# Residual rows loaded ahead of a quarter's last products, and wide weights issued by GpSimd, both in written order

## The chip, the cores and the metric

One core of a Trainium2 chip runs the whole kernel. The metric is the device time of one execution in microseconds (us), as the median of several runs; 1192.09 us for the kernel before, from three runs. A profiled execution gives one more time, its own, and a trace of every instruction. PE is TensorE, DVE VectorE, ACT ScalarE, POOL GpSimd, and SP is SyncE, which here does nothing but issue DMA transfers. POOL can issue transfers too; it then does so between its own computations.

## The reference

Two decoder layers over 1024 tokens of 1024 channels, with 256 memory tokens. Each layer projects its input, forms a main branch and a branch that attends into the memory, gates both, projects them back and normalizes the sum with the scaled input, the residual:

```python
def mixer_sublayer(x, mem, w_in, w_mem_kv, w_out, main_fn):
    h = x @ w_in
    u_main = h[..., :D_MAIN]
    q_mem = h[..., D_MAIN:D_MIX]
    g_main = h[..., D_MIX:D_MIX + D_MAIN]
    g_mem = h[..., D_MIX + D_MAIN:]
    y_main = main_fn(u_main)
    y_mem = memory_attention(q_mem, mem, w_mem_kv)
    y = jnp.concatenate([y_main * jax.nn.silu(g_main), y_mem * jax.nn.silu(g_mem)], axis=-1)
    return y @ w_out
...
    y = mixer_sublayer(x, mem, w_in[layer], w_mem_kv[layer], w_out[layer], main_fn)
    x = layer_norm(ALPHA * x + y, ln_g[layer], ln_b[layer])
```

In layer 0 `main_fn` is a causal pooling over windows of 2, 4, 8 and 16 tokens. In layer 1 it is attention with 16 heads of 64 channels, in which a cumulated forget gate is added to the logits; keys, values and gates come from one projection of layer 1's input.

## The kernel before

**Products.** Every f32 operand is split into two parts of lower precision (three with a second copy), and a product is three matmuls. Splitting a weight is work of ACT and DVE, or, while `low[0]` is set (L230, L330), of POOL alone.

**The order of the work.** The program is written for a framework that orders each engine's instructions by a priority of its own, from the order in which they are written and from when it takes their inputs to be ready. An instruction that is ready early, such as a load of weights, can be put far ahead of its place. Two things restrain it: PE's order is the written one in the attention stages (L523, L1229), and an instruction handed to `tc.keep_in_program_order` is put behind the instruction of its engine that was written last. Buffers come from pools: a tag names a shape and the number of buffers, and a load waits until a buffer of its tag is free.

**Heads of layer 1 (`fox`, L1133).** 16 heads run one after the other in eight steps each, one step for every block of 128 queries, from the last block to the first. In a step PE makes the logits (L1026, matmuls in L323), DVE adds the rows of the forget gate and takes the extremum (L1028), ACT exponentiates (L1036), ACT and DVE make two halves (L1064, L1065), and SP turns them by a DMA transpose (L1081, T<-P). Six steps later PE multiplies them with the values (L1090). POOL makes the masked diagonal three steps ahead (L1002).

**The fill.** Between these parts, PE works through projections that later heads need: keys, queries, values and gates of the next pairs. `Fill.pump` (L53) doles them out by columns. Each projection is a `slab` (L325) of 48 matmuls of 512 columns. In the fill, where `low[0]` is set, a slab first asks for its weights as one wide tile of 512 KB (L331, L332, tag B of ten buffers), then splits its first half (L335; on POOL L176, L193, L178, named B<-B, w<-B and w<-B,w), then its second (L338). The three `yield 0` let the fill start these ahead of the slab's own matmuls: the first as soon as the slab is second in line, the others when the slab in front has at most 30 and 16 matmuls left (L59). The keys' slab of each pair and a gate are started by hand in steps 2, 5 and 6 of a pair's second head (L1179 to L1182). There are 27 wide loads, all on SP. In the last pair three late gates (`late_gate`, L1121) are among the fill, and the output weights are fetched and split beside them (L1187 to L1209).

**Weights seen ahead in layer 0.** `look_ahead` (L242) loads weights of layer 1 only to take the largest magnitude. These loads are issued by POOL, in written order (L258, W<-in_win_dram and others).

**Output products and norm (`OutProj.rest`, L615).** The 1024 tokens are four quarters `sp` of 256. For each quarter three groups `c` of four weight tiles follow one another: 2, 0, 1. Each group loads its part of y (L634, T<-y0d or T<-y1d), splits it and runs 48 matmuls (L599). In layer 1 the first two quarters are interleaved. After group 1 `norm` (L650) takes the quarter's two blocks of 128 rows: it gets a G buffer, loads the residual rows (L655: x in layer 0, x1 in layer 1), adds the products to them (L659), takes mean and variance (L660, L662), scales (L670, L672) and stores (L673). In layer 0 it also splits the result into halves and turns them into X (L678). G has four buffers, one of which a piece of the output weights holds during this stage (`PG`, L138).

Of the kernel before, what the change touches and what calls it, by code (L numbers as in the profile page):

```python
# [18 lines left out]
P = 128  # L19
# [53 lines left out]
def run(units):  # L73
    for _ in units:
        pass
# [3 lines left out]
def trunk_kernel(ctx, tc, x, xT, memT, win, wk, wv0, wv, wmk, wmv, wout, poolw, pscale, lng, lnb, bforget, out):  # L79
# [5 lines left out]
    nc = tc.nc  # L85
# [18 lines left out]
    def sb(shape, tag, bufs, dt=F32, where=None):  # L104
        return (where or pool).tile(shape, dt, tag=tag, name=nm(tag), bufs=bufs)

    def ps(shape, tag, bufs):
        return psum.tile(shape, F32, tag=tag, name=nm(tag), bufs=bufs)

    def G(shape=(P, S), dt=F32):  # L110
        return sb(list(shape), "G", 4, dt)

    def T(shape=(P, S), dt=F32R):
        return sb(list(shape), "T", 6, dt)
# [10 lines left out]
    def tiny(n, dt=F32):  # L125
        return small.tile([P, n], dt, tag=f"s{n}{dt}", name=nm("s"), bufs=4 if n < 12 else 2)
# [53 lines left out]
    def parts_of(make, shape):  # L180
        return Split(make(shape), make([shape[0], 2] + list(shape[1:]), BF16))
# [7 lines left out]
    def three(a, b):  # L189
        return (a.hi, b.hi), (a.top, b.lo), (a.lo, b.hi if isinstance(a, Wide) else b.top)  # L190
# [4 lines left out]
    def hi_lo(to, src, pinned=False, top=None):  # L195

        pin = tc.keep_in_program_order if pinned else lambda ins: ins
        pin(nc.scalar.copy(to.hi, src))  # L198
        pin(nc.vector.tensor_tensor(to.lo, src, to.hi.bitcast(F32), ALU.subtract))  # L199
        pin((top or nc.scalar.copy)(to.top, src))  # L200
# [8 lines left out]
    def split_w(src_dram, shape, sc=None, r=None, pin=lambda ins: ins):  # L209
        if r is None:  # L210
            r = raw(shape)
            nc.sync.dma_start(r, src_dram)
        if sc is not None:
            to = half_of(wt, shape)
            if low[0]:
                gp_scaled_hi_lo(to, r, sc)
            else:
                scaled_hi_lo(to, r, sc, pin)
            return to
        to = parts_of(wt, shape)  # L220
        (gp_hi_lo if low[0] else hi_lo)(to, r)
        return to
# [102 lines left out]
    def slab(pieces_dram, X, evac, banks=("pj", 2), g=0):  # L325

        arrived = isinstance(pieces_dram, list)
        sc = sws[g] if isinstance(X, Half) else None
        both = (None, None)
        if low[0]:  # L330
            wide = roomy[0]([P, 2, 4, P])  # L331
            nc.sync.dma_start(wide, pieces_dram.rearrange("c p k m -> p c k m"))  # L332
            both = wide[:, 0], wide[:, 1]
            yield 0
        ws = list(pieces_dram) if arrived else [split_w(pieces_dram[0], [P, 4, P], sc, both[0])]  # L335
        if low[0]:
            yield 0
            ws.append(split_w(pieces_dram[1], [P, 4, P], sc, both[1]))  # L338
            yield 0
        accs = {}  # L340
        high, low_top = (0,), (1, 2)
        if sc is not None:
            order = [(n, pc, (0, 1, 2)) for n in range(2) for pc in range(2)]
        elif arrived:
            order = [(n, pc, part) for pc in range(2) for n, part in ((0, high), (1, high), (1, low_top), (0, low_top))]
        else:
            order = [(0, pc, part) for part in (high, low_top) for pc in range(2)]
            order += [(1, pc, part) for part in (low_top, high) for pc in range(2)]
        seen = {0: 0, 1: 0}
        for n, pc, part in order:  # L350
            if len(ws) <= pc:
                ws.append(split_w(pieces_dram[pc], [P, 4, P], sc, both[pc]))
            if n not in accs:
                accs[n] = ps([P, NH], *banks)
            for i in part:
                a, b = three(ws[pc], X)[i]
                for k in range(4):
                    seen[n] += 1
                    nc.tensor.matmul(  # L359
                        accs[n], a[:, k, :], b[:, pc * 4 + k, n * NH : (n + 1) * NH],  # L360
                        start=seen[n] == 1, stop=seen[n] == 3 * KT,
                    )
                    if seeing[0]:
                        seeing[1] += 1
                        if seeing[1] % 8 == 0:
                            look_ahead()
                    if seen[n] == 3 * KT:
                        evac(slice(n * NH, (n + 1) * NH), accs[n])
                    yield NH
# [174 lines left out]
    class OutProj:  # L544
# [70 lines left out]
        def rest(self, resid, X, dst):  # L615
            order = [(sp, c) for sp in range(ST // 2) for c in (2, 0, 1)]
            accs, splits, gb = {}, [24], []
            if self.accs:
                accs[0], order[:6], splits = self.accs, [(0, 0), (1, 2), (0, 1), (1, 0), (1, 1)], [16, 24]
            if X is not None:  # L620
                self.split(splits.pop())

            def loads():

                for v in (lng, lnb):
                    t = sb([P, D], "P", 4)
                    nc.sync.dma_start(t, v[self.l].partition_broadcast(P))
                    gb.append(t)

            for sp, c in order:  # L630
                if c == 2:
                    accs[sp] = self.open((("T", 2), ("T", 2), ("L", 3), ("O", 1))) if 0 in accs and sp == 1 else self.open()
                src, ys = T([P, 4, 2 * P], F32), parts_of(T, [P, 4, 2 * P])
                nc.sync.dma_start(src, self.yd[c, :, :, sp * 2 * P : (sp + 1) * 2 * P])  # L634
                hi_lo(ys, src)
                if splits:
                    self.split(splits.pop(0), X is None)
                if not gb and not splits:
                    loads()
                run(self.products(accs[sp], c, ys, X is None and sp == ST // 2 - 1 and c == 1))  # L640
                if X is not None and (sp, c) == (0, 0):
                    scale_of_norm(gb)
                if X is not None and c == 0 and sp:
                    scales_of_weights(sp - 1)
                if X is not None and c == 0 and sp in (1, 2):
                    keep(sp - 1)
                if c == 1:
                    norm(sp, accs.pop(sp), gb, resid, X, dst)

    def norm(sp, accs, gb, resid, X, dst):  # L650
        for a in range(2):
            s = 2 * sp + a
            rows = slice(s * P, (s + 1) * P)
            z = G()
            nc.sync.dma_start(z, resid[rows, :])  # L655
            stats = tiny(12)
            for nh in range(2):
                zn = z[:, nh * NH : (nh + 1) * NH]
                nc.vector.scalar_tensor_tensor(zn, zn, ALPHA, accs[a][nh], ALU.mult, ALU.add)  # L659
                nc.vector.bn_stats(stats[:, 6 * nh : 6 * nh + 6], zn)  # L660
            mv, v, sd, r, t = tiny(2), tiny(1), tiny(1), tiny(1), tiny(1)
            nc.vector.bn_aggr(mv, stats.rearrange("p (a b) -> p a b", a=2))  # L662
            nc.vector.tensor_scalar(v, mv[:, 1:2], LN_EPS, None, ALU.add)
            nc.scalar.activation(sd, v, AF.Sqrt)
            nc.vector.reciprocal(r, sd)
            nc.vector.tensor_scalar(t, r, r, v, ALU.mult, ALU.mult)
            nc.vector.tensor_scalar(t, t, -0.5, 1.5, ALU.mult, ALU.add)
            nc.vector.tensor_tensor(r, r, t, ALU.mult)
            for cols in (slice(0, NH), slice(NH, D)) if s == ST - 1 else (slice(0, D),):
                nc.vector.scalar_tensor_tensor(z[:, cols], z[:, cols], mv[:, 0:1], gb[0][:, cols], ALU.subtract, ALU.mult)  # L670
            for cols in (slice(0, NH), slice(NH, D)) if s == ST - 1 else (slice(0, D),):
                nc.vector.scalar_tensor_tensor(z[:, cols], z[:, cols], r, gb[1][:, cols], ALU.mult, ALU.add)  # L672
                nc.sync.dma_start(dst[rows, cols], z[:, cols])  # L673
            if X is not None:
                two = Half(*(lines[0][:, 9 + 2 * (s % 3) + e, :] for e in range(2)))
                scaled_hi_lo(two, z, sx)
                for to, half in ((X.hi, two.hi), (X.lo, two.lo)):
                    nc.sync.dma_start_transpose(to[:, :, rows], half)  # L678
# [5 lines left out]
    X = parts_of(stream, [P, KT, S])  # L684
# [110 lines left out]
    X = X1  # L795
# [501 lines left out]
```

## Time and profile before

| | us |
|---|---|
| runs, median (lowest to highest) | 1192.09 (1189.03 to 1192.14) |
| the profiled execution | 1191.01 |
| its span, first to last instruction | 1189.3 |
| mean granted TensorE clock | 0.995 of full speed |
| DMA moved | 203.89 MB, mean 171 GB/s |

The profile is read by stage. The pooling layer and its memory attention run up to some 333 us, the output products and norm of layer 0 to some 462, the projections and memory attention of layer 1 to 640, the heads from 640 to some 1062, the last output products to 1175, and the last norm to the end. A row of the groups of instructions names the line, the engine, the operation and what it writes and reads; the time after the bar is how long its engine was busy with the group, then the mean of one in ns, then the idle time of the engine in front of it and what ended it. In a row of the timeline the first two numbers are start and duration, and the bracket at the end holds the idle time in front and its releaser.

### The profile page before, as it was taken

Reading aid. Unit: us, or ns where it says so; the run is one execution under the profiler, and the core shown is the slowest. Engines: PE = TensorE matmul, PEld = TensorE weight load, DVE = VectorE, ACT = ScalarE, POOL = GpSimd, SP = SyncE. Lnnn points to the kernel's source line nnn. Section 1 sums busy time; section 2 is a strip of 40 time slices with the busy share of each in tenths; the row PEclk is TensorE's granted clock in tenths of the full one; section 3 lists DMA queues with packets and bytes.
Section 4 is the critical chain, followed back from the end, with each engine's and each line's share of the span. In section 5 each row is a group of like instructions: output and inputs, shape, how many; then the busy total and the mean of one; then the engine's idle time right before and its main releaser. Section 6 shows DMA issues by size and latency. Waiting matters only on the chain. (4 is left out here: it accounts for less than half of the span.)

```text
span 1189.3 us, 19794 instructions
## 1 busy us (share of the span) xinstructions
PE 1164.2 (98%) x6894; PEld 672.1 (57%) x6941; DVE 781.7 (66%) x1840; ACT 684.7 (58%) x1512; POOL 285.5 (24%) x437
## 2 busy tenths in 40 slices
PE   8999999999999999999999999999999999999996
PEld 5566776555555557556674555555555545455553
DVE  6744675555765566447655888778777787874654
ACT  6478875976563234557431776666766677774210
POOL 3321001310000000000002454555554445750000
PEclk8999999999999999999999999999999999999998
DMA  7576656754286544446644789989997999875530
GB/s 259 170 250 193 171 104 213 246 179 148 89 284 170 148 136 121 133 128 124 176 148 113 172 184 220 191 171 204 187 210 150 169 195 204 217 191 171 175 109 35
DMA packets 286196, 203.89 MB, mean 171 GB/s; under 512 B 224912, under 2 KB 238352, under 8 KB 286096
## 3 DMA queue, kind: packets, MB, share of 16 engines
q1 hardware_dynamic: 279696, 181.59, 60.4%
q0 software_dynamic: 6400, 21.04, 5.4%
q8 instruction: 54, 0.88, 0.3%
q14 instruction: 46, 0.38, 0.1%
HBM read 116.01 MB, written 22.61 MB: 117 GB/s over the span
## 5 line engine op out<-in xcount | busy, mean ns | idle before, releaser
L359 PE MATMUL pj<-A,w 128*128 128x512 f16 (+2 forms) x2875 | 662.3, 383 | 4.2 <-DMA A<-A 1.2
L359 PEld LDWEIGHTS <-w 128*128 128x128 f16 (+1 forms) x2560 | 245.7, 98 | 281.2 <-issue 11.3
L1036 ACT ACTIVATE T<-MK,s 128x512 f32<-128x512 f32 x192 | 111.2, 579 | 64.6 <-DVE s L1028 47.7
L1065 DVE SCALAR_TENSOR_TENSOR P<-T,s,P 128x512 f16<-128x512 f32 x192 | 112.0, 613 | 39.1 <-ACT P L1064 38.0
L1064 ACT ACTIVATE P<-T,s 128x512 f16<-128x512 f32 x192 | 103.0, 575 | 53.1 <-issue 28.9
L599 PEld LDWEIGHTS <-T 128*128 128x128 bf16 x736 | 70.6, 98 | 89.8 <-issue 4.4
L1002 POOL TENSOR_SCALAR_AFFINE_SELECT raw<-R 128x256 f32<-128x256 f32 (+3 forms) x128 | 59.4, 466 | 178.7 <-DVE s L1028 96.2
L199 DVE TENSOR_TENSOR w<-raw,w 128x512 bf16<-128x512 f32 x74 | 52.3, 708 | 54.1 <-ACT w L198 36.7
L323 PE MATMUL L<-A 128*128 128x512 f16 (+3 forms) x384 | 84.4, 326 | 3.2 <-DVE s L1028 3.1
L885 POOL MEMSET G<- 128x128 f32 x1 | 0.2, 204 | 335.5 <-DVE V L541 335.5
L359 PEld LDWEIGHTS pj<-A,w 128*128 128x128 f32 x352 | 65.1, 188 | 16.5 <-ACT w L198 1.2
L199 DVE TENSOR_TENSOR T<-T,T 128x1024 bf16<-128x1024 f32 x23 | 28.0, 1219 | 68.8 <-PE pj L599 38.3
L178 POOL TENSOR_TENSOR w<-B,w 128x512 f16<-128x512 f32 x54 | 62.8, 1165 | 4.0
L323 PEld LDWEIGHTS <-A 128*128 128x128 f16 x384 | 37.4, 98 | 46.3 <-issue 4.8
L198 ACT CAST T<-T 128x1024 fp32r<-128x1024 f32 x23 | 24.1, 1047 | 62.6 <-DMA T<-y1d 34.9
L198 ACT CAST w<-raw 128x512 fp32r<-128x512 f32 x76 | 46.7, 615 | 23.2 <-DMA raw<-in_win_dram 9.8
L1090 PEld LDWEIGHTS <-V 128*64 128x64 f16 (+1 forms) x1152 | 50.6, 104 | 12.9 <-issue 5.6
L1090 PE MATMUL O<-T,V 128*64 128x128 f16 (+1 forms) x1152 | 57.5, 220 | 0.0
L599 PE MATMUL pj<-B,T 128*128 128x512 bf16 (+1 forms) x187 | 52.1, 385 | 0.3
L1028 DVE CUSTOM_DVE_ANT_0 MK<-L,R,scales 128x512 f32<-128x512 f32 x64 | 45.3, 708 | 9.8 <-PE L L323 9.4
L200 ACT CAST w<-raw 128x512 bf16<-128x512 f32 x78 | 48.2, 618 | 3.3 <-PE pj L359 1.9
L599 PE MATMUL L<-B,T 128*128 128x512 bf16 (+1 forms) x165 | 47.0, 394 | 0.7 <-ACT T L200 0.5
(289 smaller groups left out, 1843.5 us busy)
## 6 DMA issues: line engine op xcount, KB each, us to landing
raw<-in_win_dram SPq DMA_DIRECT2D x66, 256.0 KB, 3.3
W<-in_win_dram POOLq DMA_DIRECT2D x48, 256.0 KB, 3.8
R<-cumd SPq DMA_DIRECT2D x16, 512.0 KB, 4.4
B<-in_win_dram SPq DMA_DIRECT2D x15, 512.0 KB, 5.0
y0d<-Y SPq DMA_DIRECT2D x12, 512.0 KB, 4.0
raw<-in_wout_dram SPq DMA_DIRECT2D x24, 256.0 KB, 2.7
T<-y0d SPq DMA_DIRECT2D x12, 512.0 KB, 4.5
A<-A SPq DMA_DIRECT2D x24, 256.0 KB, 4.1
```

Of the source, the lines that this page charges most:

```text
L178: pin(nc.gpsimd.tensor_tensor(to.lo, src, to.hi, ALU.subtract))
L198: pin(nc.scalar.copy(to.hi, src))
L199: pin(nc.vector.tensor_tensor(to.lo, src, to.hi.bitcast(F32), ALU.subtract))
L200: pin((top or nc.scalar.copy)(to.top, src))
L323: nc.tensor.matmul(acc, a, b, start=i == 0, stop=i == len(terms) - 1)
L359: nc.tensor.matmul(accs[n], a[:, k, :], b[:, pc * 4 + k, n * NH : (n + 1) * NH], start=seen[n] == 1, stop=seen[n] == 3 * KT,)
L599: nc.tensor.matmul(accs[a][nh], y, w, start=kt == 8 and i == 0, stop=kt == 7 and i == 2,)
L1002: tc.keep_in_program_order(nc.gpsimd.affine_select(C[:, :w], R[:, lo:up], [[-1, w]], ALU.is_ge, -NEG, base=w - P, channel_multiplier=1,))
L1036: nc.scalar.activation(e, p[:, lo:up], AF.Exp, bias=top, scale=-1.0, accum_out=sums[:, n, hd % 2, i : i + 1],)
L1064: nc.scalar.activation(pair[:, lo:up], e, AF.Copy, scale=r)
L1065: nc.vector.scalar_tensor_tensor(pair[:, L + lo : L + up], e, r, pair[:, lo:up], ALU.mult, ALU.subtract)
L1090: nc.tensor.matmul(acc[rows, (i % 4) * P : (i % 4) * P + P], v[:, b, 2 * j : 2 * j + (1 if e else 2), :].rearrange("p e d -> p (e d)"), pt ...
```

## The change

`norm` no longer asks for its rows. `rest` does it through a new function `rows_of`, for both blocks of the quarter at once, in front of the matmuls of group 1, and the loads are kept in program order on SP. The wide load of a fill slab is issued by GpSimd instead of SP, and kept in program order there.

```diff
         if low[0]:
             wide = roomy[0]([P, 2, 4, P])
-            nc.sync.dma_start(wide, pieces_dram.rearrange("c p k m -> p c k m"))
+            tc.keep_in_program_order(nc.gpsimd.dma_start(wide, pieces_dram.rearrange("c p k m -> p c k m")))
             both = wide[:, 0], wide[:, 1]
             yield 0
...
                 if not gb and not splits:
                     loads()
+                if c == 1:
+                    zs = rows_of(resid, sp)
                 run(self.products(accs[sp], c, ys, X is None and sp == ST // 2 - 1 and c == 1))
...
                 if c == 1:
-                    norm(sp, accs.pop(sp), gb, resid, X, dst)
+                    norm(sp, accs.pop(sp), gb, zs, X, dst)
 
-    def norm(sp, accs, gb, resid, X, dst):
+    def rows_of(resid, sp):
+        zs = [G() for _ in range(2)]
+        for a, z in enumerate(zs):
+            tc.keep_in_program_order(nc.sync.dma_start(z, resid[(2 * sp + a) * P : (2 * sp + a + 1) * P, :]))
+        return zs
+
+    def norm(sp, accs, gb, zs, X, dst):
         for a in range(2):
             s = 2 * sp + a
             rows = slice(s * P, (s + 1) * P)
-            z = G()
-            nc.sync.dma_start(z, resid[rows, :])
+            z = zs[a]
             stats = tiny(12)
```

## The prediction

> **What bounds the kernel now.** I read the page's first lines, then the busy time of each engine by stage, then TensorE's own waits. The columns of the stage rows are the stretch, its length, and busy time of PE, PEld, DVE, ACT and POOL, the granted clock, the DMA share and GB/s.
>
> ```profile
> span 1189.3 us, 19794 instructions
> PE 1164.2 (98%) x6894; PEld 672.1 (57%) x6941; DVE 781.7 (66%) x1840; ACT 684.7 (58%) x1512; POOL 285.5 (24%) x437
> ...
> 0.00:30.00 30.00, 26.00 (x88) 15.01 (x89) 18.59 (x36) 18.92 (x27) 11.76 (x19) 0.89 0.73 259
> 30.00:300.00 270.00, 268.42 (x1478) 168.45 (x1500) 162.53 (x321) 189.77 (x451) 43.97 (x77) 1.00 0.60 185
> 300.00:590.00 290.00, 286.18 (x1512) 167.41 (x1523) 177.28 (x360) 144.14 (x276) 0.00 (x0) 1.00 0.54 149
> 590.00:1062.00 472.00, 466.77 (x3304) 254.50 (x3302) 356.42 (x1008) 298.79 (x712) 227.41 (x340) 1.00 0.85 187
> 1062.00:1172.88 110.88, 109.86 (x489) 63.20 (x498) 54.51 (x93) 32.69 (x45) 2.36 (x2) 1.00 0.37 124
> 1172.88:1189.31 16.43, 7.01 (x32) 3.58 (x30) 12.35 (x26) 0.41 (x2) 0.00 (x0) 0.81 0.16 64
> ```
>
> TensorE is busy in 1164.2 of 1189.3 us. Of its 25 idle us, 4.0 lie in the start and 9.4 in the last norm, after the last product. All the rest, stage by stage, is 1.6 + 3.8 + 5.2 + 1.0 = 11.6 us. An order of loads can win nothing else, so the question is which of these 11.6 us belong to the loads that the change moves.
>
> ```profile
> PE L L323 <- DVE s L1028: 3.1, 6, 1.1
> PE L L599 <- ACT T L200: 1.8, 2, 1.3
> PE pj L359 <- DMA A<-A: 1.2, 1, 1.2
> PE pj L359 <- POOL w L178: 0.7, 1, 0.7
> PE pj L359 <- POOL w L193: 0.2, 1, 0.2
> ```
>
> These are five rows of TensorE's waits: total, times, longest. No row of that list names a residual row (G). Two, 0.7 and 0.2 us, name the splits of wide weights on POOL. The only one that names a DMA, A<-A, is no transpose of the heads (T<-P).
>
> **Residual rows.** Nothing is added or dropped: SP goes on issuing eight loads in each layer, two a quarter. Both are now written behind that quarter's last T load (L634), and the second moves past the store and, in layer 0, the two transposes of the quarter's first norm. The question is how late they may be.
>
> ```profile
> SPq L655 <- DMA out_dram<-G: 10.7, 3, 7.1
> ...
> 1135.03 7.94 SPq L634 DMA_DIRECT2D T<-y1d  x2
> 1154.28 0.33 SPq L655 DMA_DIRECT2D G<-x  x1
> 1172.88 0.69 DVE L659 SCALAR_TENSOR_TENSOR G<-G,L 128x512 f32<-128x512 f32 x1 [16.68 <-PE L L599]
> 1178.35 0.69 DVE L659 SCALAR_TENSOR_TENSOR G<-G,L 128x512 f32<-128x512 f32 x1
> ```
>
> The last residual load is issued at 1154.28 and is read by the L659 at 1178.35, 24 us later; residual loads land in 3.2 to 8.6 us.
>
> ```profile
> DMA to landing us min/median/max: 3.2/4.8/8.6
> ```
>
> So the rows are there 15 us before they are read, and the DVE waited for TensorE (16.68 us), not for them. What sets 1154.28 is the free G buffer: SP waits for an earlier row's store. A buffer is no sooner free when it is asked for earlier, so this load hardly moves. The T loads of the same quarter end at 1135.03 + 7.94 = 1142.97, so the new place is free of a conflict. Cost of this part: 0. Without its cover, one load late by its whole 8.6 us on the last norm would be the bound above; 24 us of room exclude it, and nothing can be gained below 0, since no wait names G. What is behind a residual load on SP are the next T loads and the stores. They are not pinned, and their stage has TensorE idle for 1.0 us only.
>
> **Wide weights: what it costs POOL.** 27 loads of 512 KB (a tile of 128 x 2 x 4 x 128 f32) leave SP's queue, where each took 0.4 to 1.5 us to issue, and go to POOL's.
>
> ```profile
> L332 SPq DMA_DIRECT2D B<-in_win_dram x15: 367/720/1467, 517.4 to 1012.9; - x15
> L332 SPq DMA_DIRECT2D B<-in_wk_dram x6: 379/392/674, 580.5 to 792.3; - x6
> L332 SPq DMA_DIRECT2D B<-in_wv_dram x6: 421/678/1069, 581.6 to 824.8; - x6
> DMA to landing us min/median/max: 3.7/5.0/8.6
> L258 POOL DMA_DIRECT2D W<-in_win_dram x48: 546/546/736, 24.9 to 231.5; - x48
> 640.00:1055.00 415.00, 410.81 (x2870) 216.85 (x2870) 322.45 (x934) 285.44 (x680) 215.61 (x326) 1.00 0.90 191
> ```
>
> The rows of L332 give the shortest, median and longest issue in ns, and the first and last start; the row of landings is that of L332 too. A POOL-issued load of 256 KB (L258) holds POOL for 0.55 us. One of 512 KB isn't in the trace: between 0.55 (one instruction is one instruction) and 1.1 (twice the rows). I take 1.1: 27 x 1.1 = 30 us on an engine that is idle for 415 - 216 = 199 us of the heads' 415. It lies beside TensorE's work; if that cover were gone, up to 30 us. What SP saves, its transposes may use to leave sooner; no wait of TensorE names them, so that is worth 0.
>
> **Wide weights: the place.** Before, SP's load could run ahead: the first three groups begin at 517 to 582, and the heads at 640. Stepping through the fill's column counts (L53 to L71, L1142 to L1221), I get for each wide load the POOL instruction that it is now written behind, and so its room: from that instruction's end to the split that needs it. The buffer is no matter: ten B tiles, and in written order the wide tile before was split by POOL itself. The tightest room is that of the v weights of pair 5, written at head 8, step 4, behind the mask that ends at 855.58:
>
> ```profile
> 855.29 0.29 POOL L1002 TENSOR_SCALAR_AFFINE_SELECT raw<-R 128x128 f32<-128x128 f32 x1 [0.39 <-DVE s L1028]
> 858.83 0.69 POOL L176 TENSOR_SCALAR B<-B,scales 128x512 f32<-128x512 f32 x1
> 860.30 1.16 POOL L178 TENSOR_TENSOR w<-B,w 128x512 f16<-128x512 f32 x1
> 869.35 0.59 PE L359 MATMUL pj<-A,w 128*128 128x512 f16 x2
> ```
>
> Asked for at 855.6 and landed after 1.1 + 5.0 = 6.1 us, at 861.7, it holds the split (L176) of 858.83, and on POOL the masks and splits behind it, for 2.9 us; with the longest landing, 8.6, for 6.5 us. The split ends at 861.46 now and its first product runs at 869.35, 7.9 us later. So TensorE doesn't see it in either case. Behind the split wait the masks that DVE's L1028 needs; they are made three steps ahead, and POOL idles in front of them anyway:
>
> ```profile
> POOL raw L1002 <- DVE s L1028: 96.2, 48, 4.4
> ```
>
> That is 2.0 us each in 48 of 128 masks, which takes up the rest. Cost: 0 with the short landing; with the long one at most the 0.7 us that a late split costs TensorE today. I take 0, by the room.
>
> One wide load gains. That of the late gate of pair 5, written at head 14, step 4, could not be issued on SP before 1012.12, behind transposes:
>
> ```profile
> 1005.41 0.29 POOL L1002 TENSOR_SCALAR_AFFINE_SELECT raw<-R 128x128 f32<-128x128 f32 x1 [0.39 <-DVE s L1028]
> 1007.68 4.38 SPq L1081 DMA_TRANSPOSE T<-P  x2
> 1012.12 1.90 SPq L332 DMA_DIRECT2D B<-in_win_dram  x2
> 1017.49 1.72 POOL L176 TENSOR_SCALAR B<-B,scales 128x512 f32<-128x512 f32 x2 [4.08 <-DMA B<-in_win_dram]
> ```
>
> POOL is free for it at 1005.70, so it lands at some 1011.8 instead of 1017.4, and the 4.08 us that POOL waited go. With them go TensorE's 0.7 and 0.2 us on L178 and L193. The gain lies between 0 (if the next split is late in its turn) and 0.9; I take 0.9, since the room of 5.6 us exceeds the wait.
>
> **The sum.** 0 + 0 - 0.9. The profiled execution took 1191.01 us (span 1189.3 and 1.7 around it), 1.1 under the median of 1192.09: 1191.0 - 0.9 = 1190.1 in its own time, **1191.2** beside the median. A difference of 0.3% (3.6 us) is about what the measurement can tell from none: the three runs lie 3.1 us apart.
>
> **Rivals.**
>
> A, slower: the second queue holds up the transposes. In eight heads a wide load is now asked for in step 4 or 5, just as the head's last needed transposes leave. In head 6 their room is short:
>
> ```profile
> L1081 SPq DMA_TRANSPOSE T<-P x2: 1298/2198/3097, 811.8 to 813.2; - x2
> DMA to landing us min/median/max: 6.4/6.6/6.8
> 820.96 1.75 PE L1090 MATMUL O<-T,V 128*64 128x128 f16 x39
> ...
> 700.00:750.00 50.00, 49.15 (x353) 26.14 (x352) 40.73 (x122) 35.59 (x89) 26.28 (x41) 1.00 0.99 201
> ```
>
> Issued at 813.2 and landed 6.4 later, at 819.6, they are read at 820.96: 1.3 us. At 201 GB/s 512 KB take 2.6 us. A delay by all of it costs 2.6 - 1.3 = 1.3 us there, and 8 x 1.3 = 10 us if all eight were as tight; half of that gives 1197 us. It decides from a delay of 1.3 us. For it: the wide loads that ran ahead come into the heads' stretch, whose DMA share is 0.90 already. Against it: up to 824.8 the heads had wide loads among their transposes before too, at a share of 0.99 between 700 and 750, and still TensorE was busy for 49.15 of those 50 us and waited for no T<-P. [...] No run here shows two loaded queues in the heads.
>
> C, slower: starved POOL issue. If a wide load needs more than 869.35 - 855.6 - 2.6 (the split) = 11.2 us, TensorE waits. At 12.5 us, and with nine loads of such room (a third, an assumption), it is 12 us: 1204. Against it: 8.6 is the longest landing, and with 1.1 it stays below. [...]
>
> B, faster: SP, no longer held by wide loads that wait for buffers, feeds everything sooner and all 5.2 idle us of 590 to 1062 go: 1186.9. For it: SP's long waits,
>
> ```profile
> SPq L332 <- POOL w L178: 31.1, 3, 26.0
> ```
>
> which end. Against it: the largest part, 3.1 us, waits for DVE's own L1028.
>
> D, it does not do what it says: the late gate is held elsewhere, and nothing moves: 1192.1.
>
> **How the numbers follow.** Forecast 0.68 (own range 1187.5 to 1194, the spread of the runs on both sides); A 0.13, C 0.06, B 0.07, D 0.06. Faster: B and a hundredth of the forecast, 0.08. Slower: A and C, 0.19. Same 0.73. The range goes from B's 1187 to 1197.5, with A's middle in it.
>
> **What would show it.** Right: L332 issues on POOL, each some microseconds before its L176; the 4.08 us before L176 and the PE waits on L178 and L193 gone; L655 of 1154 and 438 about where they were; PE busy within 1 us of 1164. Wrong: a PE wait on T<-P or L1090 (A), on L178 in many heads (C), or L599 waiting for T loads behind a residual row on SP.

## The result and the profile after

| | median of the runs, us | lowest to highest | ratio to before, 95% interval |
|---|---|---|---|
| before (22 runs) | 1191.04 | 1188.86 to 1193.15 | |
| after (22 runs) | 1195.68 | 1190.79 to 1200.9 | 1.0038 [1.0028, 1.0049] |
| after, once more (12 runs; before beside them 1190.96) | 1194.32 | 1191.18 to 1200.48 | 1.0036 [1.0019, 1.0054] |

The changed kernel is slower by some 4.5 us, and its runs lie 10 us apart where those of before lie 4. So one profile can't show the loss: the first one of the changed kernel took 1192.63 us, 1.6 more than that of before, and the second, of the repeat, 1200.03 us. Both are read here. Lines behind L655 have moved by seven: L1081 is now L1088, L1090 is L1097, L1028 is L1035.

First the page of the first profile (span, engines, queues with packets, MB and share of the 16 DMA engines), and the row of the stage windows that holds the heads:

```profile
span 1190.9 us, 19821 instructions
PE 1168.0 (98%) x6941; PEld 672.3 (56%) x6941; DVE 783.4 (66%) x1840; ACT 685.3 (58%) x1512; POOL 303.5 (25%) x464
...
q1 hardware_dynamic: 272352, 167.43, 57.0%
q0 software_dynamic: 10288, 35.20, 9.8%
...
590.00:1062.00 472.00, 465.09 (x3265) 252.20 (x3263) 356.81 (x1006) 298.81 (x711) 246.04 (x367) 1.00 0.90 193
```

The 27 loads of 512 KB, 14.16 MB, have gone from SP's queue q1 to GpSimd's queue q0 (before, from the same part of the page: 181.59 and 21.04 MB). TensorE is idle for 472 - 465.09 = 6.9 us of the heads' stretch, 1.7 more than before. The 1168.0 busy us of the whole span can't be set against the 1164.2 of before, in whose trace 47 matmuls are missing (6894 against 6941). For the same reason the idle times of 1.6 and 3.8 us that the prediction read for 30 to 590 us are too large.

Who TensorE waited for in that profile (total, times, longest):

```profile
PE L L599 <- ACT T L200: 2.8, 2, 2.3
...
PE O L1097 <- DMA T<-P: 1.6, 2, 1.3
...
PE pj L359 <- POOL w L178: 0.7, 1, 0.7
...
PE pj L359 <- POOL w L193: 0.5, 2, 0.3
```

The second row is new: products that wait for a transpose. The last two are the waits that the prediction wanted to see gone. The first row has one wait of 2.3 us behind the heads, at 1061.0, where the longest was 1.3 before; what lengthened it is not shown. In this profile the heads' first products with values begin 3.2 us sooner than before (669.8 against 673.0) and the last ones end 1.3 us sooner (1060.0 against 1061.3), so what makes its span 1.6 us longer stands behind the heads, in that wait and in a lower clock after it, of which more is said at the end. The second profile shows where a longer execution loses its time: its span, the same wait, the issue of one last transpose and of one wide load with their landing, and two stage rows of 4 us.

```profile
span 1198.3 us, 19821 instructions
...
PE O L1097 <- DMA T<-P: 6.8, 2, 3.8
```

```profile
L1088 SPq DMA_TRANSPOSE T<-P x1: 2105/2105/2105, 894.2 to 894.2; - x1
...
DMA to landing us min/median/max: 7.3/7.3/7.3
...
901.49 1.74 PE L1097 MATMUL O<-T,V 128*64 128x128 f16 x36 [2.95 <-DMA T<-P]
```

```profile
L332 POOL DMA_DIRECT2D B<-in_win_dram x1: 763/763/763, 894.2 to 894.2; - x1
...
DMA to landing us min/median/max: 5.2/5.2/5.2
```

```profile
902.00:906.00 4.00, 4.00 (x46) 3.25 (x41) 0.43 (x2) 1.45 (x4) 1.16 (x1) 0.60 0.93 189
1002.00:1006.00 4.00, 3.77 (x53) 3.60 (x54) 0.00 (x0) 0.00 (x0) 1.30 (x2) 0.60 1.14 335
```

At 894.2 GpSimd asked for a wide load and SP for the last transpose that the first products of head 9 (tiles 7 to 4) need, both at once on two queues. The transpose landed 7.3 us later, at 901.5, and TensorE stood still for 2.95 us. At head 13 it happened again, for 3.8 us, with a wide load that GpSimd had asked for 1.6 us before the transpose. In the 4 us behind each of the two waits the granted clock was 0.60 on average; by my estimate from these rows that takes 2 x 4 x 0.4 = 3.2 us more. Together that is 6.8 + 3.2 = 10.0 us. The span is 9.0 us longer than before, although the heads' first products with values began 2.4 us sooner (670.6 against 673.0).

The transposes of the heads over the whole stretch (640 to 1060 us: before, after, and the second profile of after): shortest, median and longest time in ns for which an issue holds SP, and the landing, from the start of the issue to the data:

```profile
L1081 SPq DMA_TRANSPOSE T<-P x96: 1211/1982/4212, 655.7 to 1052.4; - x96
...
DMA to landing us min/median/max: 2.8/4.8/7.3
```

```profile
L1088 SPq DMA_TRANSPOSE T<-P x96: 1211/2102/4897, 652.6 to 1052.8; - x96
...
DMA to landing us min/median/max: 2.7/5.0/10.7
```

```profile
L1088 SPq DMA_TRANSPOSE T<-P x95: 1212/2061/5500, 653.4 to 1058.2; - x95
...
DMA to landing us min/median/max: 2.7/5.5/10.7
```

The first products of a head need the transpose of its tile 4, and in heads 5 and 13 of the first profile and 9 and 13 of the second that transpose ended the wait. Of each I took from the trace when its data were ready (the end of the last DVE instruction that writes them), when SP issued it, when it landed, and when TensorE had finished what stands in front of the products:

| head, profile | issued after its data, us | landed after the issue, us | TensorE ready after the data, us | TensorE waits, us |
|---|---|---|---|---|
| 5, before | 5.3 | 4.1 | 13.4 | 0 |
| 5, after, first | 7.6 | 6.2 | 13.5 | 0.3 |
| 9, before | 5.0 | 4.4 | 13.4 | 0 |
| 9, after, second | 8.9 | 7.3 | 13.3 | 2.95 |
| 13, before | 0.4 | 4.9 | 8.6 | 0 |
| 13, after, first | 4.2 | 5.7 | 8.7 | 1.3 |
| 13, after, second | 6.3 | 7.3 | 9.9 | 3.8 |

Before, these three transposes had 4.0, 4.0 and 3.3 us to spare, and that is used up in two ways. They land 0.8 to 2.9 us later after their issue, and, which is the larger part each time, SP issues them 2.3 to 5.9 us later after their data. SP has 27 issues fewer to make and still falls behind. The transposes themselves hold it longer: their 96 issues take 202.9 us before, 216.8 and 220.9 after. Where a load of L332 is under way during the issue, one takes 2.7 us on average after the change (2.2 before), and 1.9 to 2.0 where none is (2.1 before).

On GpSimd the change shows as follows (issues of L332 in ns with their first and last start, their landing, and the late gate of pair 5 with what followed on GpSimd and on TensorE):

```profile
L332 POOL DMA_DIRECT2D B<-in_win_dram x15: 751/763/780, 594.4 to 1026.3; - x15
...
  POOL B L176: 57.7, 17
...
DMA to landing us min/median/max: 4.3/6.5/9.9
```

```profile
1007.87 0.77 POOL L332 DMA_DIRECT2D B<-in_win_dram  x1
...
1015.71 1.73 POOL L176 TENSOR_SCALAR B<-B,scales 128x512 f32<-128x512 f32 x2 [5.37 <-DMA B<-in_win_dram]
...
1018.08 1.90 PE L359 MATMUL pj<-A,w 128*128 128x512 f16 x8 [0.17 <-POOL w L193]
1020.68 1.47 PE L359 MATMUL pj<-A,w 128*128 128x512 f16 x6 [0.70 <-POOL w L178]
```

An issue costs GpSimd 0.76 us, a wide load lands in 6.5 us instead of 5.0, and GpSimd now waits 57.7 us for them in front of its splits (4.1 before). TensorE's waits on splits are 0.7 + 0.5 us, hardly changed.

### The profile page after: what moved, and what is told of

It is laid out like the page before. It is cut to its first block, busy times and chain, and to the rows that moved or that the text cites. A ratio compares the mean times of both kernels' runs of the same rounds, so it can differ in the third digit from the quotient of the medians.

```text
span 1190.9 us, 19821 instructions
## 1 busy us (share of the span) xinstructions
PE 1168.0 (98%) x6941; PEld 672.3 (56%) x6941; DVE 783.4 (66%) x1840; ACT 685.3 (58%) x1512; POOL 303.5 (25%) x464
## 5 line engine op out<-in xcount | busy, mean ns | idle before, releaser
L359 PEld LDWEIGHTS <-w 128*128 128x128 f16 (+1 forms) x2560 | 245.6, 98 | 281.2 <-issue 10.7
L1097 PE MATMUL O<-T,V 128*64 128x128 f16 (+1 forms) x1152 | 57.5, 220 | 1.6 <-DMA T<-P 1.6
L1097 PEld LDWEIGHTS <-V 128*64 128x64 f16 (+1 forms) x1152 | 50.6, 104 | 14.6 <-issue 6.2
L176 POOL TENSOR_SCALAR B<-B,scales 128x512 f32<-128x512 f32 x54 | 37.8, 702 | 58.8 <-DMA B<-in_win_dram 24.0
L1035 DVE CUSTOM_DVE_ANT_0 MK<-L,R,scales 128x512 f32<-128x512 f32 x64 | 45.3, 708 | 10.5 <-PE L L323 10.1
```

The lines of the kernel that those rows point to most:

```text
L359: nc.tensor.matmul(accs[n], a[:, k, :], b[:, pc * 4 + k, n * NH : (n + 1) * NH], start=seen[n] == 1, stop=seen[n] == 3 * KT,)
L1035: nc.vector.tensor_tensor_reduce(p[:, lo:up], lg, rows, unq, top, ALU.add, ALU.min, m[:, n : n + 1])
L1097: nc.tensor.matmul(acc[rows, (i % 4) * P : (i % 4) * P + P], v[:, b, 2 * j : 2 * j + (1 if e else 2), :].rearrange("p e d -> p (e d)"), pt ...
```

## The experiments

All start from the kernel before if nothing else is said, and all were timed beside runs of it on the same chip. Where only wide loads are moved or extra ones added, TensorE, ACT and DVE run their computations in the order of before, but for the run on ACT's queue, of which see there.

**Which part of the change?** The change with its wide loads back on SP, so that only the residual rows differ, and the kernel before with only its wide loads moved:

```diff
 rows only, from the changed kernel
-            tc.keep_in_program_order(nc.gpsimd.dma_start(wide, pieces_dram.rearrange("c p k m -> p c k m")))
+            nc.sync.dma_start(wide, pieces_dram.rearrange("c p k m -> p c k m"))
 wide loads only, from the kernel before
-            nc.sync.dma_start(wide, pieces_dram.rearrange("c p k m -> p c k m"))
+            tc.keep_in_program_order(nc.gpsimd.dma_start(wide, pieces_dram.rearrange("c p k m -> p c k m")))
```

> The residual rows alone are moved; the wide loads stay on SP and run ahead. If the rows had a part in the loss: 1193 to 1196 us, with the runs spread over some 10 us as those of the changed kernel. If the loss is that of the wide loads (held here): within 0.1% of the kernel before, 1190 to 1192 us, with its narrow spread of 4 us, and L599 waiting for nothing new.

> The wide loads alone go to GpSimd's queue in written order. If they are the cause: the whole loss, ratio 1.003 to 1.005 and runs from 1191 to 1201 us. If the rows are: 1.000.

Rows only: 1191.21 against 1190.55 us, ratio 1.0006 [0.9996, 1.0015]. Wide loads only: 1196.06, ratio 1.0056 [1.0035, 1.0078]. The whole loss is the wide loads', and their profile has the wait of the changed kernel (heads 1, 5 and 13):

```profile
PE O L1090 <- DMA T<-P: 3.5, 3, 2.5
```

**Written order, or GpSimd's queue?** The two parts of the edit apart: on GpSimd without the order, so that the loads run ahead as they did on SP, and in written order on SP.

```diff
 on GpSimd, running ahead
-            nc.sync.dma_start(wide, pieces_dram.rearrange("c p k m -> p c k m"))
+            nc.gpsimd.dma_start(wide, pieces_dram.rearrange("c p k m -> p c k m"))
 on SP, in written order
-            nc.sync.dma_start(wide, pieces_dram.rearrange("c p k m -> p c k m"))
+            tc.keep_in_program_order(nc.sync.dma_start(wide, pieces_dram.rearrange("c p k m -> p c k m")))
```

> The wide loads go to GpSimd's queue, but are not kept in written order, so that they run ahead as they did on SP. Theory queue (the second queue takes turns with the heads' transposes, whenever it is used): still slower, 1.002 to 1.005, and TensorE waits for T<-P. Theory place (the loads are asked for too late and hold GpSimd at its splits): as fast as before, 1.000, and the 57.7 us that GpSimd waits in front of L176 gone.

> The wide loads stay on SP, but in written order, so that all 27 fall into the heads. Theory queue: one queue, so as before, 0.999 to 1.001, though GpSimd may wait some 20 to 60 us at its splits. Theory place: slower by 0.3% or more, as the changed kernel, since the weights are asked for as late.

Running ahead on GpSimd: 1200.58, ratio 1.0087 [1.0068, 1.0107]. In written order on SP: 1228.14, 1.0319 [1.0306, 1.0333]. Both are worse than the change, for different reasons, and for the run on SP I had expected no loss. TensorE's longest wait in the one, and in the other, with the landing of its transposes:

```profile
PE T L323 <- DMA T<-P: 7.6, 1, 7.6
```

```profile
PE pj L359 <- POOL w L193: 27.1, 8, 7.2
...
DMA to landing us min/median/max: 2.8/4.3/7.1
```

With weights that run ahead TensorE waits for no split in the first kernel, and yet it loses 10 us: between 575 and 590 us seven wide loads on GpSimd's queue pass beside the transposes of the memory attention, and TensorE waits 7.6 us for one of these. In head 1 it waits 3.7 us more, which the list puts down to ACT; the wait ended when the transpose of tile 4 landed, 10.2 us after its issue. In the second kernel, a wide load stands behind transposes that still wait for their data (SP waits 90.6 us for DVE's L1065 in front of them), GpSimd waits 66.2 us for the loads, and the weights are late (27.1 us); but no transpose of its heads lands after more than 7.1 us. In the changed kernel late weights cost TensorE 1.2 us in all, 0.3 more than before, so lateness is not what it suffers from.

**Some of the loads.** I held that seven loads do the harm, those that the first step of a head asks for just as the head before sends its last transposes: the queries of pairs 2 to 7 and one late gate. One kernel leaves these seven on SP and puts 20 on GpSimd, the other puts only these seven there. A third keeps all 27 on GpSimd and asks for each 12 matmuls later.

```diff
 twenty (for seven, the two branches change places)
+            nc.sync.dma_start(wide, pieces_dram.rearrange("c p k m -> p c k m")) if step0 else tc.keep_in_program_order(nc.gpsimd.dma_start(wide, pieces_dram.rearrange("c p k m -> p c k m")))
 all, later (in the fill)
-                while ahead[2] > (2 if behind > 30 * NH else 1 if behind > 16 * NH else 0):
+                while ahead[2] > (3 if behind > 36 * NH else 2 if behind > 30 * NH else 1 if behind > 16 * NH else 0):
```

> All wide loads on GpSimd in written order, but for seven (queries of pairs 2 to 7 and the late gate of pair 3), which go back to SP as before. These seven are the ones asked for in step 0 of a pair's first head, within 2 us of the issue of the last transposes that the head before needs. Theory collision (these seven hold up those transposes on the second queue): most of the loss gone, 1.000 to 1.002, and TensorE no longer waits for T<-P. Theory load (any wide load on the second queue costs, wherever it stands): two thirds of the loss stay, 1.003 to 1.004. The wait of L599 at the end, some 2 us, belongs to neither and stays.

> The reverse: only the seven go to GpSimd in written order, the other twenty stay on SP as before. Theory collision: TensorE waits for T<-P as with all 27, 1.002 to 1.005. Theory load: a quarter of the loss, 1.001. The wait of L599 at the end should be as in the kernel before, 0.5 us, since the last two late gates are on SP.

> All wide loads on GpSimd, but asked for 12 matmuls of the fill later (36 left of the slab in front instead of at once); the splits stay where they are written. Theory collision: the loads fall behind the last transposes, so fewer waits for T<-P, 1.000 to 1.003, although GpSimd waits more at its splits (100 us instead of 68). Theory place (weights too late): more loss than with the wide loads alone, 1.007 or more, with TensorE waiting for L178 and L193.

Twenty: 1195.11, ratio 1.0035 [1.0022, 1.0048]. Seven: 1191.3, 1.0009 [0.9996, 1.0022]. All, later: 1198.59, 1.0063 [1.0041, 1.0085]. My theory of the seven fell: without them the loss stays, and with them alone there is none that can be told. In the profile of the twenty the wait on T<-P is 1.7 us, and the largest wait is another one, 4.4 us of the logits at 836.7. In front of it ACT waited 2.2 us for a transpose issued at 822.1, between a wide load on SP (821.5) and one on GpSimd (822.6), which landed after 14.4 us:

```profile
L1081 SPq DMA_TRANSPOSE T<-P x1: 3986/3986/3986, 822.1 to 822.1; - x1
...
  ACT P L1064: 2.2, 1
...
DMA to landing us min/median/max: 14.4/14.4/14.4
```

The next transpose held SP for 8.9 us. Moving the loads by 12 matmuls only moves the meetings: the waits are at heads 6 (1.9 us) and 13 (3.4 us; the list puts it down to ACT, but it ends 0.1 us after the landing of the transpose of tile 4).

**GpSimd's queue, or any second queue?** The wide loads in written order on ACT's queue:

```diff
-            nc.sync.dma_start(wide, pieces_dram.rearrange("c p k m -> p c k m"))
+            tc.keep_in_program_order(nc.scalar.dma_start(wide, pieces_dram.rearrange("c p k m -> p c k m")))
```

> [...] Theory second queue (two queues take turns on the DMA engines): transposes land as late as with GpSimd's (longest over 9 us), ratio 1.003 or more. Theory GpSimd's queue (its own way of issuing is what is slow or in the way): 0.999 to 1.002, and landings as on SP, 5 us.

1196.56, ratio 1.0055 [1.0037, 1.0073], as much as the wide loads alone cost on GpSimd. Its profile has only 0.5 us on T<-P, and one wait of 4.0 us for which the trace names nobody. The timeline offers one: those logits read A, and the last copy into A before them (L909) was issued on SP between two transposes and landed 2.3 us later, at 993.7.

```profile
991.36 0.46 SPq L909 DMA_DIRECT2D A<-A  x1
...
993.80 1.02 PE L323 MATMUL L<-A 128*128 128x512 f16 x4 [4.01 <-issue]
```

So here, too, a short transfer of SP probably came late. But in this kernel ACT and DVE also run some instructions in another order (84 of ACT's 1512 places and 296 of DVE's 1840 differ). Whether any second queue costs the same is not shown.

**The second queue alone.** The used wide loads stay on SP, and 27 extra loads of the same 512 KB go to a place in DRAM that nothing reads, so no weight can be late by what they wait for. They are on GpSimd, or on SP behind the wide load, or on GpSimd with 64 KB each:

```diff
-            nc.sync.dma_start(wide, pieces_dram.rearrange("c p k m -> p c k m"))
+            nc.sync.dma_start(wide, pieces_dram.rearrange("c p k m -> p c k m")); tc.keep_in_program_order(nc.gpsimd.dma_start(roomy[1](), pieces_dram.rearrange("c p k m -> p c k m")))
...
-        roomy.append(land)
+        roomy.append(land); roomy.append(lambda: dram.tile([P, 2, 4, P], F32, name=nm("spare")))
 on SP: nc.sync for nc.gpsimd; small: pieces_dram[0][:, 0, :] into [P, P]
```

> The kernel before, with every wide load on SP where it was, and 27 more loads of the same 512 KB on GpSimd's queue, each written behind the wide load and kept in program order on GpSimd; they go to a place in DRAM that nothing reads. The order of TensorE, ACT, DVE and SP is that of before, and no weight can be late through it. Theory (a second queue beside the transposes is what costs): the transposes land later when they meet an extra load (median some 6 us instead of 5.5, longest over 8), TensorE waits for T<-P, and the kernel is 2 to 8 us slower than before (ratio 1.002 to 1.007). Rival (the weights are late, or their order matters, and the second queue is innocent): no more than 1 us, ratio within 1.001.

> The contrast: the same 27 extra loads, at the same places of the program, kept in program order on SP, so that all stands in one queue; the wide loads that are used stay as before. Theory (second queue): a transpose waits at most for the extra load in front of it to be issued, 0.4 to 1.5 us, and lands in the time of before (median below 5, longest 7); TensorE does not wait for T<-P, and the ratio is within 1.002. Rival (it is only the bytes, 13.5 MB more beside the heads): as slow as the run with the extra loads on GpSimd.

> The kernel before with 27 extra loads on GpSimd's queue at the same places as in the run with 512 KB each, but of 64 KB each (an eighth): as many instructions on GpSimd and as many uses of the second queue, almost no bytes. Theory (the bytes on the second queue share the DMA engines with the transposes): an eighth of those bytes costs about an eighth of the 10 us, 1 to 2 us, ratio within 1.002, and the longest landing of a transpose stays near 7 us. Rival (GpSimd held up by issuing, or a fixed price of each use of the second queue): nearly as slow as with 512 KB, ratio above 1.005.

> The changed kernel once more, for a second profile of it. Theory (second queue): the waits on transposes are not always at the same heads; TensorE waits again for T<-P (1 to 4 us in all), at other heads than 794.8 and 992.3, and the median is 3 to 6 us above before. Rival (one fixed place is late): the same two waits at the same heads.

On GpSimd: 1201.1 against 1190.96, ratio 1.0086 [1.0069, 1.0103]. On SP: 1192.2, 1.0012 [1.0003, 1.0022]. Small, on GpSimd: 1191.12 against 1190.22, 1.0006 [0.9997, 1.0014]. The landings of the heads' transposes in the three, and TensorE's waits in the first:

```profile
DMA to landing us min/median/max: 3.2/5.6/9.0
...
PE pj L359 <- POOL w L193: 4.2, 1, 4.2
PE O L1090 <- DMA T<-P: 3.3, 3, 1.4
PE pj L848 <- DVE G L857: 2.8, 1, 2.8
```

```profile
DMA to landing us min/median/max: 2.7/5.0/8.0
```

```profile
DMA to landing us min/median/max: 2.8/5.1/7.6
```

GpSimd's 27 issues and uses of the queue cost nothing that can be told while they carry few bytes; with 512 KB each they cost 10 us, and the transposes' tail is there again. The wide loads on SP suffer as well: the late gate's weights, on SP as before, are now waited for during 4.2 us. Their load was issued at 1022.3, behind two transposes that held SP for 7.3 us instead of 4.4. The price was above the 2 to 8 us that I expected. The run on SP wasn't free of waits on T<-P as I expected either (2.2 us in its profile), though its time is as expected. The repeat of the changed kernel was read above: of its two waits one is at the head of the first profile, head 13, the other at a new one.

**One queue, or an earlier moment?** On SP the extra loads had run ahead along with the wide loads; the last for keys was asked for at 798 us, on GpSimd at 930. So I put them on SP in front of the wide load, where written order holds them among the transposes of their step, and ran those on GpSimd again beside it.

```diff
-            nc.sync.dma_start(wide, pieces_dram.rearrange("c p k m -> p c k m"))
+            tc.keep_in_program_order(nc.sync.dma_start(roomy[1](), pieces_dram.rearrange("c p k m -> p c k m"))); nc.sync.dma_start(wide, pieces_dram.rearrange("c p k m -> p c k m"))
```

> 27 extra loads of 512 KB into a place in DRAM that nothing reads, as in the run with them on GpSimd, but on SP, written in front of the wide load and kept in program order, so that each stands among the transposes of its own step (up to 1030 us, as on GpSimd) instead of running ahead. The used wide loads stay on SP and run ahead as before. Theory (two queues at once delay transposes that were asked for earlier; in one queue a load stands behind them): longest landing of a transpose at most 8 us, ratio within 1.003. Rival (it is the moment of the load, beside the transposes, on whatever queue): T<-P waits of 3 us and more, ratio 1.006 to 1.010, as on GpSimd.

> The 27 extra loads of 512 KB on GpSimd's queue once more, beside the run with them on SP in written order. Both theories: 8 to 12 us slower than before, transposes landing up to 9 us and more. Second queue: at least 6 us slower than the run with them on SP; rival: the same within 3 us.

On SP in written order: 1195.7 against 1190.77, ratio 1.0037 [1.0023, 1.0052]. On GpSimd: 1203.43, 1.0099 [1.0072, 1.0126]. First the issues, the landings of the transposes and the wait on them with SP, then the same with GpSimd:

```profile
L332 SPq DMA_DIRECT2D spare<-in_wk_dram x6: 582/591/1057, 679.9 to 934.6; - x6
...
DMA to landing us min/median/max: 3.2/5.3/8.1
...
PE O L1090 <- DMA T<-P: 2.6, 2, 1.6
```

```profile
L332 POOL DMA_DIRECT2D spare<-in_wk_dram x6: 656/664/679, 673.0 to 931.7; - x6
...
DMA to landing us min/median/max: 2.8/5.8/11.0
...
PE O L1090 <- DMA T<-P: 6.6, 4, 2.4
```

Both theories hold a part. Of the 12.7 us that the extra loads cost on GpSimd (by the medians, of six runs each), 4.9 come on SP too, at much the same places, most of them some us later: that is 14.16 MB more, read and written, beside the transposes, on whatever queue, and it is more than I allowed. The other 7.7 us come with the second queue. Not all of it is waits on T<-P: 4.9 us of the run on GpSimd are one wait for the late gate's weights (2.5 in that on SP). How the 4.5 us of the change itself, which adds no bytes, divide between moment and queue, was not measured; the run with loads that run ahead on GpSimd shows that the queue can cost without late loads, though it moves them too.

The two groups can also be told apart by transposes. Of each one in the heads I took issue and landing from the trace, and how long a load of L332 was under way meanwhile; "meets" are those with over 1.5 us of it, "alone" those with at most 0.3. (A transpose that takes longer has more time to meet a load, so the rows say more than the columns.)

| | alone: median us | meets: number, median, longest |
|---|---|---|
| before | 4.4 | 24, 5.5, 6.9 |
| after, first and second profile | 4.4, 4.4 | 42, 6.2, 10.7; 44, 6.8, 10.7 |
| extra loads on GpSimd, both runs | 4.3, 4.3 | 58, 6.6, 9.0; 56, 6.5, 11.0 |
| extra loads on SP, ahead; in written order | 4.4; 5.2 | 39, 5.9, 8.0; 55, 5.6, 8.0 |

A transpose without a load beside it takes 4.4 us in the kernel after as in the one before; the 5.2 us with extra loads on SP in written order are not explained. One that meets a load on its own queue takes 5.5 to 5.9, on another queue 6.2 to 6.8 with a tail to 11; and the change has nearly doubled the meetings.

One effect of the change goes the other way. The heads' first products with values begin at 669.0 to 670.6 us in the seven profiles in which none of the wide loads runs ahead into the memory attention (after twice, wide loads only, in written order on SP, twenty, later, on ACT's queue), and at 672.2 to 673.6 in the five in which they all run ahead on SP and no load of 512 KB is on GpSimd. That gain of some 2 to 3 us stands in front of the heads and is less than what is lost in them; which wait it comes from is not shown.

No version here beats the kernel before: the residual rows alone come nearest, between 0.04% faster and 0.15% slower.

## Why the prediction was wrong

**The direction was wrong, the time within the range.** 1191.2 was forecast and 1195.68 measured. The range reached that far only for rival A. "Slower", by a little more than 0.3%, had 0.19.

**Residual rows, 0: right.** 1.0006 [0.9996, 1.0015]. The last loads were issued at 436.94 and 1156.27 us, against 438.63 and 1154.28 before, the one of 1156.27 for the reason given, the free buffer: SP waited 2.3 us for a store in front of it.

**Issue on GpSimd, 1.1 us each, hidden: right.** It is 0.76 us, between the bounds and below the value taken, and 27 small extra issues cost at most 0.14%.

**The place, 0: right in its result.** GpSimd waits more than forecast, since a wide load lands in 6.5 us and not in 5.0, but TensorE's waits on splits went only from 0.9 to 1.2 us. Rival C's starved issue did not come: no run shows its 12.5 us, and the longest issue and landing of the first profile, 0.78 and 9.9 us, stay below its 11.2.

**The gain, -0.9: wrong.** The step said that GpSimd is free for the late gate at 1005.70, behind the mask. It issued at 1007.87, because the next mask (1006.14) and two splits of output weights stood between, and the load took 7.75 us. So it landed at 1015.6 instead of 1011.8, GpSimd waited 5.37 us instead of 4.08, and both waits of TensorE stayed.

**What SP's transposes gain, "worth 0", and the case against rival A: the step that failed.** The step let SP's transposes leave sooner, or at worst as before, and the sum has no term for what the loads do to them; I left that to rival A, at 0.13. The runs show the opposite: those of tile 4 in heads 5, 9 and 13 were issued 2.3 to 5.9 us later after their data where TensorE waited for them, and landed 0.8 to 2.9 us later after their issue. TensorE's waits on T<-P are 0 before, 1.6 and 6.8 us after. Against A stood that wide loads had passed among the transposes before, at a DMA share of 0.99, without a wait. That row was read rightly and proves little here: those loads shared the transposes' queue, and the change ends just this. In one queue the transposes that met a load took 5.5 us and at most 6.9; in two, 6.2 to 6.8 and up to 10.7. A's mechanism is one part of what happened; the other, SP held longer by the issues, it did not have. Its 1197 us lies 1.3 above the time, which is partly luck. Its place was wrong: I looked at even heads, where a load is asked for in step 4 or 5, and the waits are at odd heads, 5, 9 and 13, whose last transposes meet the load of the next head's first step. That room, 4.0, 4.0 and 3.3 us, I had not computed, and A's largest delay of 2.6 us would not have used it up.

How the two queues share the DMA engines is a guess of the expectations that no run shows; what the traces show is times. In the second profile a transpose asked for in the same instant as a wide load on the other queue landed 7.3 us later, and the extra loads, kept in program order, leave the longest landing of a transpose at 8.1 us on its own queue and at 11.0 on GpSimd's.

**The size** is the waits and their echo: in the second profile 6.8 us of waits and, by the estimate above, 3.2 us of lower clock. The clock was in no term of the sum, nor in A's. In the first profile 1.6 us of waits on T<-P go with a wait of 2.3 us behind the heads, for which no cause is shown.

## What to carry to other kernels

In this kernel loads cost the transposes less in the transposes' own queue than on another: 27 extra loads of 512 KB, in written order, cost 4.9 us in SP's queue and 12.7 us on GpSimd's, although GpSimd was busy for only 235 of the 472 us from 590 to 1062. Before a load is moved to another queue, list which short transfers will then meet it and how much room each has, counted from its data to its reader, since the issue can come late as well as the landing; a busy share that was harmless in one queue, 0.99 here, doesn't answer that. And look at the granted clock behind a stall of TensorE: behind those of 2.95 and 3.8 us it was 0.60 over 4 us, by estimate 1.6 us more for each.

## What the runs showed of the hardware

**The clock behind a short stall.** In the 4 us behind the waits of 2.95 and 3.8 us in the second profile the granted clock was 0.60 on average, and behind one of 2.3 us at 1061.0 in the first profile it was 0.59. Behind a wait of 1.9 us it was 0.60 in one run (all, later) and 1.00 in another (extra loads on SP), and behind one of 2.5 us it was 1.00 (wide loads only). In this order, as stage rows of 4 us, the waits of 2.3, 1.9, 1.9 and 2.5 us:

```profile
1063.00:1067.00 4.00, 3.70 (x11) 1.40 (x12) 2.42 (x3) 3.56 (x6) 0.00 (x0) 0.59 0.00 0
```

```profile
823.00:827.00 4.00, 4.00 (x41) 3.02 (x36) 1.99 (x4) 2.52 (x5) 3.83 (x6) 0.60 1.18 252
```

```profile
696.40:700.40 4.00, 3.80 (x60) 3.00 (x61) 2.37 (x5) 2.61 (x5) 2.85 (x4) 1.00 0.79 139
```

```profile
995.00:999.00 4.00, 3.79 (x60) 3.04 (x61) 1.75 (x3) 2.54 (x5) 2.46 (x3) 1.00 1.08 323
```

So between 1.9 and 2.5 us it went either way; what decides is not shown. Where it is 0.60 over 4 us, the wait costs some 1.6 us on top, by the same estimate. That may be part of why the runs of the changed kernel spread over 10 us.

**GpSimd's issue grew far less than the bytes:** 0.57 us for 64 KB and 0.66 for 512 KB where the target is DRAM (the extra loads), 0.55 for 256 KB (L258) and 0.76 for 512 KB (L332) where it is a tile on the core.

**The issue of a DMA transpose held SP longer while a load of L332 was under way:** 2.7 us on average against 1.9 to 2.0 without one, in both profiles of the changed kernel; before, 2.2 against 2.1.
